# A decoder step on one core: ten of sixteen expert column blocks as a dense product, the sample's weighted rows spread over the picking, the last layer norm tile by tile

## The chip, the cores and the metric

The kernel runs on one core of one Trainium2 chip. The metric is the device time of one launch in microseconds, the median of several runs. The profile is one further execution, recorded by the hardware profiler; its span is the time from the first to the last instruction of the program.

The core has five engines with instruction streams of their own: TensorE (PE; its weight loads are listed apart as PEld), VectorE (DVE), ScalarE (ACT), GpSimd (POOL) and SyncE (SP). Each works through its stream in order and waits on semaphores for the others. SP's stream issues plain transfers; POOL's issues the gathers, in which a list of 128 row numbers picks 128 rows of a table.

## The reference

One layer of a decoder for a prompt of 256 tokens and a sample of 8 x 4 = 32 tokens: an input projection, an RWKV head group and a sparse-attention head group, an output projection with layer norm, and then the channel mixer, a product-key expert layer (PEER) with a second layer norm. The change lies in the last part:

```python
hv, hix = lax.top_k(s, P_TOPK)
cand = (hv[:, :, 0, :, None] + hv[:, :, 1, None, :]).reshape(n, P_HEADS, P_TOPK * P_TOPK)
cand_e = (hix[:, :, 0, :, None] * N_KEYS + hix[:, :, 1, None, :]).reshape(n, P_HEADS, P_TOPK * P_TOPK)
tv, tpos = lax.top_k(cand, P_TOPK)
expert = jnp.take_along_axis(cand_e, tpos, axis=-1)
gate = jax.nn.softmax(tv, axis=-1).astype(x.dtype)
...
h = jax.nn.gelu(jnp.einsum('cd,chkd->chk', xb, u_tab[eb]), approximate=False)
return jnp.einsum('chk,chkd->cd', gb * h, v_tab[eb])
```

Each token picks 8 heads x 16 = 128 of 16384 experts. For each it needs the dot product of its row (2048 columns) with the expert's row of `peer_u`, a GELU, a gate, and the sum of the experts' rows of `peer_v` with these weights. The result is added to the token and normed: `layer_norm(DEEPNORM_ALPHA * x + f, ln2_g, ln2_b)`.

## The kernel before

The first 1200 us or so compute everything up to the choice of the experts, and the sample's own dot products; the change leaves them as they are. Tile sizes are written into the code. A planner of the framework orders the instructions of each engine by a timeline of its own, with priorities in the order of the program; instructions passed to `pin` (`tc.keep_in_program_order`) keep their order among themselves, and `tc.issue_after(i)` lets an instruction be issued only after `i`. A pool's named tile with `bufs=n` has n buffers in turn: a new tile waits until the one n before has been read for the last time. Memory of a closed pool goes to later pools, and the first writer of a new tile waits for the last reader of what lay there.

Four stages follow for the prompt's 256 tokens.

**Dense** (`dense`, lines 1873 to 1888, called 128 times from line 1891). The 2048 columns of `peer_u` are split in 16 column blocks of 128. The last `NDB` = 9 are multiplied for all 16384 experts and all tokens on TensorE, in 128 blocks of 128 experts: `ph` (128 experts x 256 tokens) sums over the nine column blocks. Three of them (`NSP` to `NDB`) are plain f32 matmuls with `Xfd` (line 1879), which run in two passes, with two weight loads and two matmuls each. The other six (`SPLIT`, in two groups of three) are split into a high part `uh`, cast on ACT (line 1639), and a rest `ul`, made on DVE (line 1640), and take three matmuls each with the split tokens `XHd`, `XLd` (line 1886). ACT then copies `ph` into the table `AW` (line 1888). A block's weights `ur` come with one transfer of 576 KB.

The other seven column blocks (`UG` = 896 columns) are not multiplied densely: for each prompt tile `t` (128 tokens) and each of a token's 128 choices, `fetch` (line 1789) gathers the 128 chosen rows, cut to 896 columns, into one of the five `rows` buffers (`NRW`), and `dot` (line 1797) multiplies them with the tokens on DVE and sums (line 1803): 256 dot products. Two of them are done before the dense stage; in each block of it `n_` = 1 or 2 follow the block's last `ul`, `NDN` = 4 of 8 blocks having the second. `table` (line 1808) lays the finished sums and the experts' numbers down by token in `TB`.

**Picking** (from line 1993, 68 steps `s_`, all pinned but for the transfers and the last norm). A step takes four tokens. `pick` compares the experts' numbers with a row of counts (`oo`, DVE, line 1918) and transposes one half on TensorE (`pt`, line 1922; ACT copies it, line 1924); `picked` takes the dense sums with it from `AW` (`px`, line 1930); one step later `product_of` reduces them on DVE to the chosen experts' sums (four small passes, line 1941), every second step adds the gathered part (line 1944) and ACT takes the GELU (line 1945); then the gate (`gated`, DVE, line 1949), three steps later the scaling (`scaled`, ACT, line 1955), and four steps later `put`, which multiplies the weights out into a dense table of 256 tokens x 16384 experts (`pa`, line 1963) that ACT writes over `AW` (line 1964). The dot products left over from the dense stage are spread over the steps 0 to 27.

In the steps 28 to 59 `smp_fetch` gathers the sample's rows of `peer_v`, two halves of 4 KB a row, into two of the same five `rows` buffers, and two steps later (30 to 61) `smp_add` multiplies them with the sample's weights `ws` into `fs`: four matmuls of 32 output rows and 512 columns, in two passes (line 1982). 32 such products make the sample's sum. After the steps the sample's sum is added to its tokens and normed in `norm_quarters` (lines 2027, 2028 and 1444 to 1459: statistics on DVE, a small matmul `avg4`, an inverse root in some ten small DVE steps, one pass on ACT and two on DVE), and 16 small transfers on SP's queue store it.

**V** (lines 2063 to 2106). The weights in `AW` are multiplied with the first `FD` = 1408 columns of `peer_v`, in 128 row blocks `k`. Each is loaded by `rows_load` on SP's queue (three buffers: every third one in the pool `vr`, the others in `vp`, which lies where the dot products' and the picking's tiles lay), split on ACT and DVE into `vh` and `vl` (two buffers each), and multiplied for both prompt tiles `t` into six banks `acc` in 18 matmuls. The other 640 columns are gathered (`row_fetch`) and summed on DVE (`row_add`, line 2058). Row block 0 is loaded at step 50 of the picking, the blocks 1 and 2 after it.

**End** (lines 2109 to 2133). `last_sum` adds the banks and the gathered part to the tokens and takes statistics; then both tiles' mean and inverse root are made together (13 small steps), and for each of the eight pieces of 512 columns ACT scales and shifts, DVE multiplies with `ln2_g` and adds `ln2_b`, and SP stores.

## Time and profile before

| | |
|---|---|
| median of 3 runs | 2496.15 us (2490.72 to 2497.42) |
| the profiled execution | 2498.71 us |
| its span | 2496.9 us |
| PE busy | 2246.1 us (90%) |
| DVE busy | 1851.9 us (74%) |
| POOL busy | 1373.4 us (55%) |
| ACT busy | 927.4 us (37%) |
| moved by DMA | 684.23 MB, 274 GB/s |

Times in rows are counted from the start of the span. A row of the timeline gives start, duration, engine, line, operation and the tiles written and read; `x6` means six such instructions in a row, and the brackets at its end give the idle time of the engine ahead of it and what ended it. Rows of the stretches give the busy time of each engine in a stretch, with the number of instructions in brackets, the TensorE clock granted (1.00 is full speed), the busy share of the DMA engines and what they moved. Matmuls overlap in their pipeline, so a busy TensorE need not be one at its peak: how far their starts lie apart tells more. A group's row gives line, engine, operation, tiles, shapes and number, then busy time and the mean in ns of one, then the idle time before it.

### The profile page before, as it was taken

The numbers are of one execution on the slowest core, as the hardware profiler recorded it, in microseconds if no ns is written. First come the engines' busy times: TensorE is split into PE (matmuls) and PEld (weight loads), VectorE is DVE, ScalarE is ACT, GpSimd is POOL, SyncE is SP. The second block draws the span as 40 slices with busy tenths as digits, with TensorE's granted clock in tenths as the row PEclk, the third lists the DMA queues.
The fourth block names the chain that finished last, engine by engine and source line by source line (L and its number), as shares of the span: only waits on it lengthen the run. The fifth ranks groups of instructions, "written<-read, shape, count | busy, mean of one in ns | idle before, by whom it ended". The sixth has DMA issues, their size and how long they took to land.

```text
span 2496.9 us, 44823 instructions
## 1 busy us (share of the span) xinstructions
PE 2246.1 (90%) x16396; PEld 1888.6 (76%) x16396; DVE 1851.9 (74%) x4241; ACT 927.4 (37%) x1848; POOL 1373.4 (55%) x1422
## 2 busy tenths in 40 slices
PE   7979999988889997789699999996699799999996
PEld 7967898875545665678598889986676688888785
DVE  5789756554563446889977776779976799988888
ACT  4433222213441333220233343434566444443433
POOL 5677423242444005478655555556656488876662
PEclk9999999998896896899899999997899899999998
DMA  7777975457668884797499999996678599999995
GB/s 219 234 235 232 272 220 172 122 178 223 214 206 269 283 299 148 282 325 241 144 385 372 370 361 357 353 336 221 216 249 294 221 369 356 362 365 361 350 358 186
DMA packets 327613, 684.23 MB, mean 274 GB/s; under 512 B 82270, under 2 KB 200992, under 8 KB 326464
## 3 DMA queue, kind: packets, MB, share of 16 engines
q1 hardware_dynamic: 246176, 342.58, 41.4%
q0 software_dynamic: 81216, 338.78, 38.4%
q8 instruction: 129, 2.11, 0.3%
q14 instruction: 92, 0.75, 0.1%
HBM read 665.69 MB, written 23.88 MB: 276 GB/s over the span
## 4 chain that ended last, share of the span: by engine, by line
PE 60%; DVE 17%; DMA 8%; issue 7%; ACT 4%; POOL 3%; SPq 1%; DVEq 0%; POOLq 0%; ACTq 0%
PE pb L2085 17%; PE ph L1886 10%; PE pj L426 8%; PE ph L1879 3%; PE pa L1668 3%; PE p L1083 2%; DVE rows L1803 2%; DMA co<-in_cache_cmp_kv,gidx 2%; DVE sr L1559 2%; PE pa L1963 2%; DVE ul L1640 2%; PE ss L1500 1%; PE px L1930 1%; PE fs L1982 1%; DVE oo L1918 1%
## 5 line engine op out<-in xcount | busy, mean ns | idle before, releaser
L457 POOL DMA_INDIRECT rows<-in_peer_u_g,gi x256 | 332.3, 1298 | 239.5 <-DVE rows L1803 195.2
L457 POOL DMA_INDIRECT rq<-in_peer_v_g,gi x256 | 378.6, 1479 | 141.8 <-DVE fP L2058 80.2
L1803 DVE SCALAR_TENSOR_TENSOR rows<-rows,x1a 128x896 f32<-128x896 f32 x256 | 272.0, 1092 | 2.9 <-DMA rows<-in_peer_u_g,gi 2.7
L1886 PE MATMUL ph<-XHd,ul 128*128 128x256 f32 x768 | 225.3, 294 | 27.6 <-DVE ul L1640 22.7
L426 PE MATMUL pj<-XH,wl 128*128 128x288 f32 (+1 forms) x752 | 230.1, 306 | 15.2 <-DVE wl L421 9.1
L426 PE MATMUL pj<-XH,wh 128*128 128x288 f32 (+1 forms) x752 | 228.2, 304 | 13.6 <-DVE ss L756 6.9
L1886 PE MATMUL ph<-XHd,uh 128*128 128x256 f32 x768 | 236.7, 308 | 0.0
L2058 DVE SCALAR_TENSOR_TENSOR fP<-rq,ge,fP 128x640 f32<-128x640 f32 x254 | 223.8, 881 | 5.9 <-DMA rq<-in_peer_v_g,gi 3.4
L426 PE MATMUL pj<-XL,wh 128*128 128x288 f32 (+1 forms) x752 | 224.5, 299 | 0.0
L1640 DVE TENSOR_TENSOR ul<-ur,uh 128x384 fp32r<-128x384 f32 x256 | 131.8, 553 | 120.1 <-ACT uh L1639 93.3
L1886 PE MATMUL ph<-XLd,uh 128*128 128x256 f32 x768 | 217.4, 283 | 0.0
L2085 PE MATMUL pb<-vl,ah 128*128 128x512 f32 (+1 forms) x768 | 207.8, 378 | 1.4 <-issue 0.5
L2085 PE MATMUL pb<-vh,ah 128*128 128x512 f32 (+1 forms) x768 | 188.0, 380 | 20.9 <-ACT vh L2077 20.9
L2085 PE MATMUL pb<-vh,al 128*128 128x512 f32 (+1 forms) x768 | 205.7, 376 | 0.0
L419 ACT CAST wh<-wraw 128x512 fp32r<-128x512 f32 (+1 forms) x188 | 114.7, 617 | 223.7 <-PE pj L426 169.0
L1879 PE MATMUL ph<-Xfd,ur 128*128 128x256 f32 x768 | 187.6, 380 | 1.1 <-DMA ur<-in_peer_u_t 1.1
L1886 PEld LDWEIGHTS ph<-XHd,ul 128*128 128x128 f32 x768 | 147.0, 192 | 42.1 <-DVE ul L1640 41.8
L2085 PEld LDWEIGHTS pb<-vh,ah 128*128 128x128 f32 x768 | 145.5, 196 | 43.8 <-ACT vh L2077 24.5
L480 DVE SCALAR_TENSOR_TENSOR CA<-co,wbc,CA 128x256 f32<-128x256 f32 x248 | 133.9, 577 | 45.5 <-DMA co<-in_cache_cmp_kv,gidx 45.2
L2085 PEld LDWEIGHTS pb<-vl,ah 128*128 128x128 f32 x768 | 145.2, 195 | 24.5 <-DVE vl L2078 4.5
L426 PEld LDWEIGHTS pj<-XH,wl 128*128 128x128 f32 (+1 forms) x752 | 142.6, 190 | 26.6 <-DVE wl L421 12.7
L1888 ACT COPY AW<-ph 128x256 f32<-128x256 f32 x128 | 77.8, 608 | 228.1 <-PE ph L1886 198.7
(854 smaller groups left out, 5472.6 us busy)
## 6 DMA issues: line engine op xcount, KB each, us to landing
ur<-in_peer_u_t SPq DMA_DIRECT2D x128, 576.0 KB
wraw<-in_w_in SPq DMA_DIRECT2D x152, 256.0 KB
cw<-in_w_out SPq DMA_DIRECT2D x32, 512.0 KB
wraw<-in_w_out SPq DMA_DIRECT2D x32, 512.0 KB
wraw<-in_peer_wq SPq DMA_DIRECT2D x32, 512.0 KB
cw<-in_peer_wq SPq DMA_DIRECT2D x32, 512.0 KB
wraw<-in_w_in SPq DMA_DIRECT2D x64, 128.0 KB
co<-in_state_win_kv SPq DMA_DIRECT2D x16, 512.0 KB
```

The source lines that it names most:

```text
L419: sc.copy(wh[:, :, :n], w[:, :, :n])
L426: last[2] = pe.matmul(pb[:n, :nt], wi[:, k, :n], xi[(o + k) // 8][:, (o + k) % 8, :nt], start=(o + k == 0 and wi is wh and xi is xh), stop ...
L457: gp.indirect_dma_start(out=dst, out_offset=None, in_=rows_, in_offset=bass.IndirectOffsetOnAxis(ap=ix, axis=0))
L480: ve.scalar_tensor_tensor(d_, x_, w_, d_, op0=OP.mult, op1=OP.add)
L1640: return ve.tensor_tensor(xl, pb, xh.bitcast(F32), OP.subtract)
L1668: pe.matmul(acc[t], xi[:, e, P * t:P * t + P], wi[:, e, :], start=(k == e == n_ == 0), stop=(k == 6 and e == 1 and n_ == 2))
L1803: i_ = ve.scalar_tensor_tensor(r_, r_, 1.0, X1a[t], op0=OP.mult, op1=OP.mult, accum_out=h_)
L1879: pe.matmul(ph[:, :NPR], w[:, e, :], Xfd[:, e - NSP, :], start=(e == NSP), stop=False)
L1886: mm = pe.matmul(ph[:, :NPR], wi[:, e - e0, :], xi[:, e, :], start=False, stop=(e == NSP - 1 and wi is wl))
L1888: return lo_, mm, sc.copy(AW[:, i1 // 64, :, i1 % 64], ph[:, :NPR])
L2058: ve.scalar_tensor_tensor(fP[t], r_, w_, fP[t], op0=OP.mult, op1=OP.add)
L2085: pe.matmul(acc[3 * t + q][:, :n_], wi[:, P * t:P * t + P], xi[:, 512 * q:512 * q + n_], start=(k == 0 and wi is ah and xi is vh), stop=(k ...
```

## The change

Five edits, all in the expert layer:

- `NDB` is 10: ten column blocks are multiplied densely, four of them plain, and the gathered rows are `UG` = 768 columns. A block's transfer is 640 KB.
- `NDN` is 6: six of eight blocks of the dense stage have a second dot product. Of the tile `uh` there are two buffers instead of three.
- In the picking's steps 0 to 27 the rows of a dot product are fetched at most two ahead (`ahead=2`), not five. The sample's 32 products stand at the steps 5, 6, 8, 10, 12, 13 and so on to 59, four in seven steps, and their fetches two steps ahead of each. The loads for the sample's norm move from step 46 to 44.
- The sample's sum, norm and stores stand in the program behind step 61 instead of after the picking.
- In V the last two row blocks are multiplied together, first both for tile 0 and then both for tile 1. The last norm makes mean and inverse root for each tile on its own, and each piece takes two operations on DVE, (x - mean) x g and that x the inverse root + b, and none on ACT.

```diff
-NDN = 4
+NDN = 6
...
-NDB = 9
+NDB = 10
...
-            wh, wl = (dp([P, e1 - e0, P], nm, F32R, bufs=3) for nm in ("uh", "ul"))
+            wh, wl = (dp([P, e1 - e0, P], nm, F32R, bufs=n_) for nm, n_ in (("uh", 2), ("ul", 3)))
...
+    turns = {5 + j * 7 // 4: j for j in range(32)}
...
-            dot(-(-left * (s_ + 1) // 28) + 2 * P - left - got[1], keep=True)
-        elif s_ < 60:
-            smp_fetch(s_ - 28)
-        if 30 <= s_ < 62:
-            smp_add(s_ - 30)
-        if s_ == 46:
+            dot(-(-left * (s_ + 1) // 28) + 2 * P - left - got[1], keep=True, ahead=2)
+        if s_ + 2 in turns:
+            smp_fetch(turns[s_ + 2])
+        if s_ in turns:
+            smp_add(turns[s_])
+        if s_ == 44:
...
+        if s_ == 61:
+            ve.scalar_tensor_tensor(x_, x_, ALPHA, fs, op0=OP.mult, op1=OP.add)
+            norm_quarters(x4p, x_, gs_, bs_, "pb")
+            for q in range(4):
+                for i in range(4):
+                    sy.dma_start(outs[1][:, i, 512 * q:512 * q + 512], x_[32 * q + 8 * i:32 * q + 8 * i + 8, :])
...
-    ve.scalar_tensor_tensor(x_, x_, ALPHA, fs, op0=OP.mult, op1=OP.add)
-    norm_quarters(x4p, x_, gs_, bs_, "pb")
-    for q in range(4):
-        for i in range(4):
-            sy.dma_start(outs[1][:, i, 512 * q:512 * q + 512], x_[32 * q + 8 * i:32 * q + 8 * i + 8, :])
...
+        parts[k] = (ah, al, vh, vl)
         for t in range(2):
-            for wi, xi in ((ah, vh), (ah, vl), (al, vh)):
...
+            for k_ in (k,) if k < P - 2 else (k - 1, k) if k == P - 1 else ():
+                ah, al, vh, vl = parts[k_]
+                for wi, xi in ((ah, vh), (ah, vl), (al, vh)):
...
     for t in range(2):
         for q in range(3):
             last_sum(t, q)
+        v_, r_ = v2[:, t:t + 1], rr2[:, t:t + 1]
         ve.bn_aggr(out=mv2[:, t, :], in_=sf[:, t].rearrange("p a b -> p (a b)"))
-    m_, v2 = mv2[:, :, 0], vp([P, 2], "v2")
-    ve.tensor_scalar(v2, mv2[:, :, 1], 1e-5, None, op0=OP.add)
-    rsqrt(vp, rr2, v2, "ln2")
-    ve.scalar_tensor_tensor(v2, m_, -1.0, rr2, op0=OP.mult, op1=OP.mult)
-    for t in range(2):
-        for q in range(4):
-            c_ = slice(512 * q, 512 * q + 512)
-            x_ = xo[t][:, c_]
-            sc.activation(x_, x_, AF.Identity, bias=v2[:, t:t + 1], scale=rr2[:, t:t + 1])
-            ve.tensor_tensor(x_, x_, g2_[:, c_], OP.mult)
-            ve.tensor_tensor(x_, x_, b2_[:, c_], OP.add)
+        ve.tensor_scalar(v_, mv2[:, t, 1:2], 1e-5, None, op0=OP.add)
+        m_ = mv2[:, t, 0:1]
+        ve.tensor_scalar(m_, m_, -1.0, None, op0=OP.mult)
+        xs_ = [(xo[t][:, 512 * q:512 * q + 512], slice(512 * q, 512 * q + 512)) for q in range(4)]
+        rsqrt(vp, r_, v_, f"ln2{t}")
+        for x_, c_ in xs_:
+            ve.scalar_tensor_tensor(x_, x_, m_, g2_[:, c_], op0=OP.add, op1=OP.mult)
+            ve.scalar_tensor_tensor(x_, x_, r_, b2_[:, c_], op0=OP.mult, op1=OP.add)
             sy.dma_start(outs[0][0, t * P:(t + 1) * P, c_], x_)
```

More of the change, by code (lines that the diff above doesn't have):

```diff
@@ L2060, in row_add @@
             ve.tensor_scalar(fP[t], r_, w_, None, op0=OP.mult)
-    acc = [bank() for _ in range(6)]
+    acc, parts = [bank() for _ in range(6)], {}
     done = 0
@@ L2080, in hybrid_decode_step @@
             ld_ = rows_load(k + 3)
+        parts[k] = (ah, al, vh, vl)
         for t in range(2):
-            for wi, xi in ((ah, vh), (ah, vl), (al, vh)):
-                for q in range(3):
-                    n_ = min(512, FD - 512 * q)
-                    pe.matmul(acc[3 * t + q][:, :n_], wi[:, P * t:P * t + P], xi[:, 512 * q:512 * q + n_],
-                              start=(k == 0 and wi is ah and xi is vh), stop=(k == P - 1 and wi is al))
+            for k_ in (k,) if k < P - 2 else (k - 1, k) if k == P - 1 else ():
+                ah, al, vh, vl = parts[k_]
+                for wi, xi in ((ah, vh), (ah, vl), (al, vh)):
+                    for q in range(3):
+                        n_ = min(512, FD - 512 * q)
+                        pe.matmul(acc[3 * t + q][:, :n_], wi[:, P * t:P * t + P], xi[:, 512 * q:512 * q + n_],
+                                  start=(k_ == 0 and wi is ah and xi is vh), stop=(k_ == P - 1 and wi is al))
         while done < min(len(queue), len(queue) * (k + 1) // (P - 2)):
@@ L2117, in hybrid_decode_step @@
     last_sum(1, 3)
+    v2 = vp([P, 2], "v2")
     for t in range(2):
```

## The prediction

> **What bounds the kernel now.** I read the stretches first (columns: stretch and length; busy time and instructions of PE, PEld, DVE, ACT, POOL; granted TensorE clock; DMA share; GB/s), because the change touches three stages with different limits.
>
> ```profile
> 1250.00:1675.00 425.00, 420.15 (x2807) 383.92 (x2806) 304.24 (x607) 165.55 (x350) 238.62 (x185) 1.00 0.98 365
> 1682.00:1815.00 133.00, 89.92 (x532) 82.82 (x531) 127.91 (x396) 60.87 (x164) 81.40 (x63) 0.78 0.70 219
> 1820.00:1940.00 120.00, 119.00 (x938) 85.29 (x938) 83.00 (x339) 81.34 (x223) 67.83 (x59) 1.00 0.78 266
> ```
>
> The dense stage (first row) is TensorE's: 2807 matmuls, 24 an expert block (three plain columns in two passes each, 18 of the split kind), are 117 blocks in 425 us, 3.63 us a block. The first 28 steps of the picking (second row) are VectorE's, busy 127.9 of 133 us, and TensorE runs there at a clock of 0.78. The other steps (third row) are TensorE's again, 119 of 120 us at full clock, with VectorE at 83. So a column moved to TensorE is paid in the first row, the dot products it shortens are earned in the second, and the sample's products, which fill the third, can be moved into the second.
>
> **The dense stage.** The timeline, PEld, ACT and DVE rows around two blocks:
>
> ```profile
> 1472.13 1.18 PEld L1879 LDWEIGHTS ph<-Xfd,ur 128*128 128x128 f32 x6
> ...
> 1473.66 0.19 PEld L1886 LDWEIGHTS ph<-XHd,ul 128*128 128x128 f32 x1
> ...
> 1475.57 1.18 PEld L1879 LDWEIGHTS ph<-Xfd,ur 128*128 128x128 f32 x6
> ...
> 1475.89 0.59 ACT L1888 COPY AW<-ph 128x256 f32<-128x256 f32 x1 [2.83 <-PE ph L1886]
> 1476.28 0.93 ACT L1639 CAST uh<-ur 128x384 fp32r<-128x384 f32 x2
> 1476.84 1.03 DVE L1640 TENSOR_TENSOR ul<-ur,uh 128x384 fp32r<-128x384 f32 x2 [2.07 <-ACT uh L1639]
> ...
> 1477.45 0.19 PEld L1886 LDWEIGHTS ph<-XHd,ul 128*128 128x128 f32 x1 [0.27 <-DVE ul L1640]
> ...
> 1479.36 1.17 PEld L1879 LDWEIGHTS ph<-Xfd,ur 128*128 128x128 f32 x6
> ```
>
> One block takes 3.44 us (1472.13 to 1475.57), the next 3.79. In the short one the first `ul` product comes 1.53 us after the block's start, in the long one 1.88: ACT evacuates the block before, only then casts `uh`, DVE then makes `ul`, and TensorE, through with its three plain columns, waits. Six weight loads in 1.18 us make a plain column 0.39. The fourth one therefore costs 0.39 us of work, but it stands ahead of the wait: TensorE reaches the first `ul` at 1.53 + 0.39 = 1.92, when `ul` is there (1.88). Every block then takes 3.44 + 0.39 = 3.83, against 3.63 on average: +0.20 x 128 = **+26 us**. Bounds: not below this (no block takes less than the short one and the fourth column's work), and 0.39 x 128 = +50 if each wait stays as long as it is. The cover is thin, 0.04 us. I take +26.
>
> `uh` with two buffers instead of three: the cast of a block's second half now waits until the second half of the block before has been multiplied, some 0.1 us before that block ends. Behind it on ACT stands at most the evacuation, and `ul` of the second half is wanted nine products of 0.12 us after the 1.92: over 2 us of room, so nothing. DVE: two `ul` (1.03) and 1.75 dot products instead of 1.5, each shorter: under 2.8 of 3.83 us. DMA: a block's load grows from 590 to 655 KB, the rows from 1.5 x 459 to 1.75 x 393 KB: 1343 KB in 3.83 us is 351 GB/s, against 365 in the row. Nothing. Of the 256 dot products two are done before this stage and 1.5 x 128 in it, so 62 are left for the picking; with 1.75 x 128 it is 30.
>
> **The first 28 steps of the picking.** VectorE's timeline, whose second row shows where one step begins and the last where the next does; below them step 28's pick, and the page's groups of two row sizes:
>
> ```profile
> 1682.25 1.22 DVE L1918 TENSOR_TENSOR oo<-CT,TB 128x1024 f32<-128x1024 f32 x1
> ...
> 1701.26 1.22 DVE L1918 TENSOR_TENSOR oo<-CT,TB 128x1024 f32<-128x1024 f32 x1
> ...
> 1703.81 1.08 DVE L1803 SCALAR_TENSOR_TENSOR rows<-rows,x1a 128x896 f32<-128x896 f32 x1
> ...
> 1704.82 1.09 DVE L1803 SCALAR_TENSOR_TENSOR rows<-rows,x1a 128x896 f32<-128x896 f32 x1
> ...
> 1706.84 1.22 DVE L1918 TENSOR_TENSOR oo<-CT,TB 128x1024 f32<-128x1024 f32 x1
> ```
> ```profile
> 1815.62 1.22 DVE L1918 TENSOR_TENSOR oo<-CT,TB 128x1024 f32<-128x1024 f32 x1
> ```
> ```profile
> L1803 DVE SCALAR_TENSOR_TENSOR rows<-rows,x1a 128x896 f32<-128x896 f32 x256 | 272.0, 1092 | 2.9 <-DMA rows<-in_peer_u_g,gi 2.7
> L2058 DVE SCALAR_TENSOR_TENSOR fP<-rq,ge,fP 128x640 f32<-128x640 f32 x254 | 223.8, 881 | 5.9 <-DMA rq<-in_peer_v_g,gi 3.4
> ```
>
> A step without dots is 2.55 us (1701.26 to 1703.81), a dot 1.01 start to start. 28 x 2.55 + 62 x 1.01 = 134.0 against 133.4 measured (1682.25 to 1815.62): the account closes. A dot of 768 elements lies midway between 896 and 640, 0.105 us less: 0.91. After: 28 x 2.55 + 30 x 0.91 = 98.7.
>
> Fourteen of the 32 sample products now fall into these steps. TensorE, in a steady step of today's second part:
>
> ```profile
> 1874.15 0.66 PE L1922 MATMUL pt<-CT,oo 128*128 128x128 f32 x4
> 1874.64 1.06 PE L1963 MATMUL pa<-oo 128*128 128x128 f32 x8
> 1875.54 1.16 PE L1930 MATMUL px<-AW,oT 128*128 128x128 f32 x8
> 1876.63 1.06 PE L1982 MATMUL fs<-rows,ws 128*32 128x512 f32 x8
> 1877.62 0.66 PE L1922 MATMUL pt<-CT,oo 128*128 128x128 f32 x4
> ```
>
> 3.47 us with a sample product, 0.99 of it that product, 2.48 without. The 28 steps ask 28 x 2.48 + 14 x 0.99 = 83.3 us of TensorE, under VectorE's 98.7. As the limits are now close I add what today's second part loses against its sum: 33 steps from 1819.82 to the last pick (1940.33, below) are 3.65 each, not 3.47, 5%: 103.6, **-30 us**. Bounds: -35 without that loss, and the rivals.
>
> **The other steps.**
>
> ```profile
> 1819.82 1.22 DVE L1918 TENSOR_TENSOR oo<-CT,TB 128x1024 f32<-128x1024 f32 x1 [0.43 <-PE pa L1963]
> ```
> ```profile
> 1940.33 1.22 DVE L1918 TENSOR_TENSOR oo<-CT,TB 128x1024 f32<-128x1024 f32 x1
> ```
>
> From step 28 to the last pick 124.7 us pass. After, 18 of these 35 steps hold a sample product (3.47) and 17 fall to VectorE's 2.55 (ACT's 81.3 us over the 33 steps are 2.46 each, just below): 105.8, with 5% 111: **-14**, bounds -19 and 0, the last if the four engines, all near 2.5 in a short step, keep each other waiting.
>
> **The start of the last stage.**
>
> ```profile
> 1952.42 0.81 ACT L1457 ACTIVATE x1a<-x1a,smv,srr 128x512 f32<-128x512 f32 x1 [0.94 <-DVE smv L1442]
> ...
> 1954.71 6.01 SPq L2031 DMA_DIRECT2D out<-x1a  x16
> ...
> 1961.09 0.37 SPq L1990 DMA_DIRECT2D v__20899<-in_peer_v  x1
> ...
> 1962.79 0.96 POOL L457 DMA_INDIRECT rq<-in_peer_v_g,gi  x1 [30.07 <-DMA out<-x1a]
> ...
> 1967.30 2.10 PEld L2085 LDWEIGHTS pb<-vh,ah 128*128 128x128 f32 x6 [5.94 <-ACT vh L2077]
> ```
>
> Sixteen stores of the sample's result stand on SP's queue ahead of the second row block's load, which leaves at 1961.09; TensorE waits 5.9 us for it. The sample's sum and norm now follow step 61, two steps after the last sample product (step 59), so the stores should be issued while the picking ends, and the load be back in time. What is late next is the cast of the first block, which today stands on ACT behind the sample's scaling at 1952.42: some 2 us earlier. Against this, the norm's VectorE work (four passes of 512, some twenty small steps, near 6 us, part of which runs among the picks already) and its one small product on TensorE, which waits for VectorE with the next transposes and puts behind it, now stand among steps 61 to 65: +2. Net **-6**, bounds 0 (the scheduler leaves the norm late) and -10.
>
> **The end.**
>
> ```profile
> 2479.78 0.38 DVE L2121 BATCH_NORM_AGGREGATE mv<-sf 128x2 f32<-128x24 f32 x2
> ...
> 2483.61 1.40 DVE L2131 TENSOR_TENSOR AW<-AW 128x512 f32<-128x512 f32 x2 [0.88 <-ACT AW L2130]
> ...
> 2490.94 2.49 DVE L2132 TENSOR_TENSOR AW<-AW 128x512 f32<-128x512 f32 x4
> ```
> ```profile
> 1967.00:2474.00 507.00, 494.12 (x2285) 430.31 (x2286) 456.89 (x455) 212.65 (x189) 375.35 (x253) 1.00 0.95 352
> ```
>
> VectorE closes this: 16 passes from 2483.61 to 2493.43, before them 2.95 us of small steps and 0.88 of waiting for ACT. In the last stage a matmul takes 494.12 / 2285 = 0.216 us, a tile's nine 1.9. Multiplied tile by tile, tile 0 is whole up to one such turn earlier (if the last block's casts, now wanted a turn earlier, come in time); the wait for ACT goes (-0.9); but the small steps, now for each tile, are done twice (+2.8) and the 16 passes stay 16. -1.9 - 0.9 + 2.8 = **0**, bounds -3 and +3.
>
> **Sum.** 26 - 30 - 14 - 6 + 0 = -24. The profiled execution took 2498.7 us (span 2496.9), 2.6 over the median; against the median, 2496.15 - 24 = **2472 us**. With the better bounds it is 26 - 35 - 19 - 10 - 3 = -41, 2455.
>
> **Rivals.** *The column is paid in full.* If a dot stands before `ul` on VectorE, the wait in front of `ul` moves along with the column: +50 in place of +26, 2496. For it: the 0.04 us of cover. Against it: in the row at 1476.84 VectorE had been idle for 2.07 us. 0.12.
>
> *The shared row buffers.* Dots and sample rows now take turns in five buffers, and a row's gather waits in POOL's one queue for the buffer five back, at times for a sample product at the end of the very step before its use; behind it wait all later gathers. The latency of one gather:
>
> ```profile
> 1691.22 1.09 DVE L1803 SCALAR_TENSOR_TENSOR rows<-rows,x1a 128x896 f32<-128x896 f32 x1 [1.08 <-DMA rows<-in_peer_u_g,gi]
> ```
>
> Here VectorE stood 1.08 us for a row. At one such place per sample product, 15 x 1.1 = +16 less what the 5% hold already: about 2485. Counting through the buffers I find it at one place in seven steps, so 0.17.
>
> *The clock.* Now the slower side: with its filling thinned out in the second part, and gaps left in the first, TensorE could get there the clock that it gets now in the first, 0.78. The work, 83.3 + 104.6 us at full clock, would take 241 in place of 258: -17, so 26 - 17 - 6 = +3, 2499; at 0.70 it is 268, +30, 2526. It decides below 0.79. Against it: a TensorE that slows becomes the bound, is busy without gaps, and the third row of the first fence shows such a stretch at 1.00. 0.11. [...]
>
> *The change doesn't do what it says*: the norm isn't run among the picks, or the steps keep their order of waits; -6 and some of -14 are missing, 2485. 0.05.
>
> **How the numbers follow.** Forecast 0.55 (2455 to 2482), buffers 0.17, full column 0.12, clock 0.11, misplaced norm 0.05. About 0.3%, 7.5 us, is what a measurement of this kernel can tell from no change, so faster means below 2488.6: forecast, buffers and misplaced norm, 0.77. Within 0.3%: 0.09 of the full column and 0.04 of the clock, 0.13. Slower: 0.03 of the full column, with a worse term beside it, and 0.07 of the clock, 0.10. The range goes from 2455, the better bounds, to 2494; outside stay the clock, half of the full column and 0.03 below.
>
> **What would show it.** Dense: plain weight loads in eights, 3.83 us apart, and no PEld wait for `ul`; 4.1 would be the first rival. Picking: first 28 steps near 104 us with VectorE still busiest, TensorE's clock over 0.9; waits of dots for their gathers would be the second rival. The rest near 111 us in two kinds of steps. The second row block's load leaving before the first is multiplied. Wrong altogether if the two gains of the picking don't come to over 26 us together.

## The result and the profile after

The changed kernel takes 2508.4 us (median of 12 runs, 2498.9 to 2517.4) against 2492.8 of the kernel before (12 runs, 2474.2 to 2498.0): a ratio of 1.0077, interval 1.0058 to 1.0095. It is slower by 0.8%; the forecast was 1% faster. The profiled execution took 2508.9 us, with a span of 2507.1.

The two profiles, cut at the same marks (first plain weight load of the dense stage, last block's, picks 0, 28 and 63, last multiplication of V):

| stretch | before, us | after, us | forecast | measured |
|---|---|---|---|---|
| up to the dense stage | 1189.9 | 1178.9 | | (-11.0) |
| its first 17 blocks | 87.6 | 101.1 | +26 in all | +13.5 |
| its other 110 blocks | 401.2 | 427.6 | | +26.4 |
| last block to pick 0 | 3.5 | 5.3 | | +1.7 |
| first 28 steps | 133.4 | 134.7 | -30 | +1.3 |
| other steps | 124.7 | 113.6 | -14 | -11.1 |
| last pick to V's last multiplication | 534.2 | 523.8 | -6 | -10.4 |
| end | 22.4 | 22.1 | 0 | -0.3 |
| sum without the first row | 1307.0 | 1328.1 | -24 | +21.1 |

The first row is no effect of the change: over the profiles of this study it lies between 1170.4 and 1200.2 us, at nine columns 1184.0 to 1198.4 and at ten 1170.4 to 1200.2. So stretches are compared here, and sums without it; the 21.1 is 0.8% of the whole, as the ratio says.

The stretches of the changed kernel (columns as in the prediction's first fence): dense stage, step 0, steps 1 to 27, the others, V.

```profile
1275.00:1700.00 425.00, 425.00 (x2851) 401.70 (x2850) 281.46 (x598) 168.09 (x329) 192.87 (x188) 1.00 0.95 344
1713.00:1728.00 15.00, 3.88 (x14) 2.79 (x14) 10.84 (x24) 0.59 (x1) 12.12 (x10) 0.53 0.86 280
1728.00:1847.00 119.00, 83.62 (x628) 65.62 (x628) 89.33 (x324) 60.53 (x164) 71.99 (x56) 0.94 0.69 217
1850.00:1960.00 110.00, 102.13 (x820) 81.02 (x819) 86.77 (x357) 80.97 (x223) 41.44 (x33) 1.00 0.54 167
1976.00:2484.00 508.00, 496.25 (x2299) 432.56 (x2299) 458.19 (x458) 212.96 (x189) 376.31 (x254) 1.00 0.95 351
```

The third row is the surprise: in 119 us VectorE is busy for 89 and TensorE for 84. Before, VectorE filled this stage (127.9 of 133). The dots did get fewer and shorter, but no engine bounds the stage any more: something is waited for. The page's group of the dots says what:

```profile
L1803 DVE SCALAR_TENSOR_TENSOR rows<-rows,x1a 128x768 f32<-128x768 f32 x256 | 244.8, 962 | 31.0 <-DMA rows<-in_peer_u_g,gi 27.1
```

Before, 2.9 us of idle time stood in front of the dots in the whole kernel; now it is 31.0, and 27.1 of it ended with the gather of a row. The view of waits in steps 1 to 27 (total us, times, longest) shows who waits for whom:

```profile
POOL rows L457 <- DVE rows L1803: 31.3, 17, 2.6
...
DVE rows L1803 <- DMA rows<-in_peer_u_g,gi: 19.2, 12, 3.6
```

A circle: POOL waits for dots to free row buffers, dots wait for POOL's gathers. One turn of it, on POOL (`in_peer_u_g` is a dot's row, `in_peer_v` a half of a sample row), then on VectorE and on TensorE:

```profile
1779.10 0.95 POOL L457 DMA_INDIRECT rows<-in_peer_v,gi  x1 [0.30 <-issue]
1781.59 1.69 POOL L457 DMA_INDIRECT rows<-in_peer_v,ig  x1 [1.53 <-DVE rows L1803]
1783.59 0.95 POOL L457 DMA_INDIRECT rows<-in_peer_u_g,gi  x1 [0.30 <-PE pa L1963]
...
1789.66 1.69 POOL L457 DMA_INDIRECT rows<-in_peer_v,gi  x1 [2.60 <-DVE rows L1803]
...
1796.73 1.69 POOL L457 DMA_INDIRECT rows<-in_peer_u_g,gi  x1 [2.07 <-PE fs L1982]
```
```profile
1783.78 0.95 DVE L1803 SCALAR_TENSOR_TENSOR rows<-rows,x1a 128x768 f32<-128x768 f32 x1
...
1788.43 0.96 DVE L1803 SCALAR_TENSOR_TENSOR rows<-rows,x1a 128x768 f32<-128x768 f32 x1 [3.68 <-issue]
```
```profile
1795.11 1.34 PE L1982 MATMUL fs<-rows,ws 128*32 128x512 f32 x8
```

The sample's gather at 1781.59, the second half of the row begun at 1779.10, waited 1.53 us for a dot. Behind it in POOL's queue stood the gather of the next dot, which left at 1783.59; the dot ran at 1788.43, 4.84 us later, after 3.68 us in which VectorE did nothing (the view calls the wait "issue", but the buffer it reads is the one gathered at 1783.59). At 1796.73 it is a dot's gather that waits, 2.07 us, for a sample product (the one at 1795.11) to free its buffer. Thirteen dots of steps 1 to 27 wait like this, 22.9 us together: the 19.2 above and this 3.68.

Step 0 is the second surprise, 15.0 us in place of 4.3:

```profile
1712.82 1.22 DVE L1918 TENSOR_TENSOR oo<-CT,TB 128x1024 f32<-128x1024 f32 x1
...
1717.45 0.96 DVE L1803 SCALAR_TENSOR_TENSOR rows<-rows,x1a 128x768 f32<-128x768 f32 x1 [1.52 <-DMA rows<-in_peer_u_g,gi]
...
1721.74 0.96 DVE L1803 SCALAR_TENSOR_TENSOR rows<-rows,x1a 128x768 f32<-128x768 f32 x1 [1.30 <-DMA rows<-in_peer_u_g,gi]
...
1727.85 1.22 DVE L1918 TENSOR_TENSOR oo<-CT,TB 128x1024 f32<-128x1024 f32 x1
```

Ten dots stand between the first two picks, two of the picking's thirty and eight of the dense stage's, and TensorE has little to do (3.9 of 15 us in the second row above).

The dense stage in the changed kernel (PEld), and the start of V (SP's queue, then PEld):

```profile
1501.14 1.61 PEld L1879 LDWEIGHTS ph<-Xfd,ur 128*128 128x128 f32 x8
...
1505.02 1.61 PEld L1879 LDWEIGHTS ph<-Xfd,ur 128*128 128x128 f32 x8
```
```profile
1958.74 5.82 SPq L2028 DMA_DIRECT2D out<-x1a  x16
1964.92 0.37 SPq L1990 DMA_DIRECT2D v__21027<-in_peer_v  x1
```
```profile
1975.46 1.17 PEld L2090 LDWEIGHTS pb<-vh,ah 128*128 128x128 f32 x6 [2.67 <-ACT ah L2076]
```

Behind the first 17 blocks nearly every block takes 3.88 us, and none waits for `ul`. The second row block's load leaves at 1964.92, 10.5 us ahead of the first multiplication; before, it left 6.0 us behind it.

### The profile page after: what moved, and what is told of

It reads as the page before. It is cut to its first block, busy times and chain, and to the rows that moved or that the text cites. A ratio compares the mean times of both kernels' runs of the same rounds, so it can differ in the third digit from the quotient of the medians.

```text
span 2507.1 us, 45293 instructions
## 1 busy us (share of the span) xinstructions
PE 2257.3 (90%) x16652; PEld 1919.0 (77%) x16652; DVE 1828.2 (73%) x4254; ACT 933.7 (37%) x1840; POOL 1328.2 (53%) x1422
## 4 chain that ended last, share of the span: by engine, by line
PE 63%; DVE 13%; DMA 10%; issue 5%; POOL 5%; ACT 2%; SPq 1%; DVEq 0%; POOLq 0%; ACTq 0%
PE pb L2090 19%; PE ph L1886 10%; PE ph L1879 8%; PE pj L426 7%; DMA rows<-in_peer_u_g,gi 3%; PE pa L1668 2%; DVE sr L1559 2%; PE p L1083 2%; DMA co<-in_cache_cmp_kv,gidx 2%; DMA big<-in_state_rwkv 2%; PE pa L1963 1%; PE px L1930 1%; PE ss L1500 1%; PE pt L1922 1%; DVE CA L480 1%
## 5 line engine op out<-in xcount | busy, mean ns | idle before, releaser
L457 POOL DMA_INDIRECT rows<-in_peer_u_g,gi x256 | 272.3, 1064 | 283.8 <-DVE rows L1803 257.1
L1803 DVE SCALAR_TENSOR_TENSOR rows<-rows,x1a 128x768 f32<-128x768 f32 x256 | 244.8, 962 | 31.0 <-DMA rows<-in_peer_u_g,gi 27.1
L1640 DVE TENSOR_TENSOR ul<-ur,uh 128x384 fp32r<-128x384 f32 x256 | 142.1, 557 | 157.6 <-ACT uh L1639 157.6
L1879 PE MATMUL ph<-Xfd,ur 128*128 128x256 f32 x1024 | 245.0, 382 | 4.0 <-DMA ur<-in_peer_u_t 4.0
L1639 ACT CAST uh<-ur 128x384 fp32r<-128x384 f32 x256 | 130.9, 513 | 309.1 <-PE ph L1886 288.3
L426 PE MATMUL pj<-XH,wl 128*128 128x288 f32 (+1 forms) x752 | 231.5, 308 | 13.5 <-DVE wl L421 7.8
L1886 PE MATMUL ph<-XHd,ul 128*128 128x256 f32 x768 | 218.5, 285 | 23.9 <-DVE ul L1640 23.9
L1879 PEld LDWEIGHTS ph<-Xfd,ur 128*128 128x128 f32 x1024 | 187.1, 192 | 25.8 <-DMA ur<-in_peer_u_t 4.7
L426 PEld LDWEIGHTS pj<-XH,wl 128*128 128x128 f32 (+1 forms) x752 | 144.4, 192 | 24.1 <-DVE wl L421 11.1
```

Source lines behind the costliest of these rows:

```text
L426: last[2] = pe.matmul(pb[:n, :nt], wi[:, k, :n], xi[(o + k) // 8][:, (o + k) % 8, :nt], start=(o + k == 0 and wi is wh and xi is xh), stop ...
L457: gp.indirect_dma_start(out=dst, out_offset=None, in_=rows_, in_offset=bass.IndirectOffsetOnAxis(ap=ix, axis=0))
L1639: sc.copy(xh, pb)
L1640: return ve.tensor_tensor(xl, pb, xh.bitcast(F32), OP.subtract)
L1803: i_ = ve.scalar_tensor_tensor(r_, r_, 1.0, X1a[t], op0=OP.mult, op1=OP.mult, accum_out=h_)
L1879: pe.matmul(ph[:, :NPR], w[:, e, :], Xfd[:, e - NSP, :], start=(e == NSP), stop=False)
```

## The experiments

"A" is the theory that dots and sample rows take each other's row buffers, "B" that the eight left-over dots hold up step 0, "C" that clock or contention does it, "D" that the two `uh` buffers slow the first blocks of the dense stage. All runs, with the sum of their profile behind the first row of the table above (before: 1307.0):

| run | ratio to before, interval | first 28 steps, us | sum, us |
|---|---|---|---|
| changed kernel | 1.0077, 1.0058 to 1.0095 | 134.7 | 1328.1 |
| e1_dense_only | 1.0077, 1.0045 to 1.0110 | 110.7 | 1319.4 |
| e2_spread_only | 1.0237, 1.0202 to 1.0272 | 204.4 | 1355.9 |
| e3_after_ahead5 | 1.0149, 1.0105 to 1.0192 | 141.4 | 1337.6 |
| e4_after_late | 1.0058, 1.0034 to 1.0082 | 112.0 | 1318.2 |
| e5_after_one | 1.0034, 1.0011 to 1.0056 | 118.7 | 1313.6 |
| e6_spread_one | 1.0087, 1.0060 to 1.0113 | 172.5 | 1325.7 |
| e7_uh2_only | 1.0036, 1.0011 to 1.0062 | 132.6 | 1310.8 |
| e8_norm_early | 0.9975, 0.9953 to 0.9996 | 132.5 | 1300.1 |
| e9_best9 | 0.9995, 0.9972 to 1.0018 | 133.6 | 1299.7 |
| e10_best8 | 0.9974, 0.9948 to 1.0000 | 140.2 | 1298.7 |
| e11_after_one5 | 1.0251, 1.0213 to 1.0289 | 137.1 | 1361.8 |
| e12_norm_end | 0.9982, 0.9957 to 1.0007 | 132.6 | 1299.7 |

### Ten columns alone

Against the kernel before:

```diff
-NDN = 4
+NDN = 6
-NDB = 9
+NDB = 10
-            wh, wl = (dp([P, e1 - e0, P], nm, F32R, bufs=3) for nm in ("uh", "ul"))
+            wh, wl = (dp([P, e1 - e0, P], nm, F32R, bufs=n_) for nm, n_ in (("uh", 2), ("ul", 3)))
```

> Only the tenth column goes to TensorE (with the two uh buffers it needs); the sample's sums, the norm and the end stay as before, so the ring of five row buffers serves dots alone in the first 28 steps and dots are fetched five ahead. Theory A (in the changed kernel the sample's rows in the dots' ring make the dots wait): without them the first 28 steps fall to what VectorE's sum says, 28 x 2.55 + 38 dots x 0.91 = 106, plus the 5 us of gaps that before had: 106 to 111 us, and the kernel is 28.9 + 1.7 (dense stage, first pick) - 25 = +5 us, ratio 1.000 to 1.005. Theory B (the eight dots left over from the dense stage choke step 0 by themselves): step 0 stays at 15 us with its waits, first 28 steps 110 to 115. Theory C (a slower granted TensorE clock or contention of the gathers, not the ring): the first 28 steps stay near 134 us and the kernel is 30 us slower, ratio 1.012.

The stretches step 0 and steps 1 to 27:

```profile
1731.00:1746.00 15.00, 3.67 (x14) 2.58 (x14) 10.45 (x22) 0.59 (x1) 12.25 (x10) 0.55 0.81 268
1746.00:1841.00 95.00, 66.50 (x510) 60.76 (x511) 89.20 (x326) 58.94 (x160) 47.24 (x30) 0.96 0.43 130
```

VectorE does the same work as in the changed kernel, 89.2 us, but in 95 us instead of 119, and no dot of steps 1 to 27 waits for its gather. These steps take 95.2 us; VectorE's account of the prediction, 27 x 2.55 + 28 x 0.91, gives 94.3. So A holds for 24 us, and B holds too: step 0 takes 15.45 us with no sample row anywhere near. C is not quite settled by this run: the sample's gathers, and what they might do to the others, are gone from the stage along with the sharing, and dots are fetched five ahead instead of two. e3 and e5 below keep those gathers. The whole is slower than expected, since the dense stage costs +36.7 (first 17 blocks 97.9, the others 427.6), not the +28.9 that I had read from two times on the clock, with the first row of the table in them.

### The spread sums alone

Against the changed kernel; `uh` has three buffers and the end is as before, too:

```diff
-NDN = 6
+NDN = 4
-NDB = 10
+NDB = 9
...
```

> The sample's sums are spread over the picking, dots are fetched two ahead and the norm follows step 61, as in the changed kernel; nine columns on TensorE and the end stay as before. Theory A (shared ring): 62 dots of 1.01 keep VectorE at 134 us in the first 28 steps, and the waits of dots for gathers that stand behind a sample row's add 15 to 30 us: 150 to 165. The other steps take 114 as in the changed kernel (-11), the last stage -10: together between -5 and +10 us, ratio 0.998 to 1.004. Theory C (no harm by the ring; the waits of the changed kernel come from its dense stage's left-over dots): first 28 steps 134 to 138, and the kernel is 17 to 21 us faster, ratio 0.992 to 0.993.

Waits of the first 28 steps:

```profile
POOL rows L457 <- DVE rows L1803: 67.8, 37, 3.9
DVE rows L1803 <- DMA rows<-in_peer_u_g,gi: 58.4, 20, 5.4
```

With 62 dots in the ring instead of 38 the same edit costs 71 us (204.4 against 133.4) where 15 to 30 were expected: a miss in size, in A's direction. The other steps (113.7) and V (510.8) are as in the changed kernel.

### The lead of the dots

Against the changed kernel:

```diff
-            dot(-(-left * (s_ + 1) // 28) + 2 * P - left - got[1], keep=True, ahead=2)
+            dot(-(-left * (s_ + 1) // 28) + 2 * P - left - got[1], keep=True)
```

> The changed kernel, with dots fetched five ahead as before instead of two. If the short lead of two dots is what makes them wait (theory A1), the first 28 steps fall from 134.7 towards 106 to 115 us and the kernel is 20 to 28 us faster than the changed one, ratio to the kernel before 0.997 to 1.000. If five buffers are too few for dots and sample rows together whatever the lead (theory A2), a row's gather still waits for the use of the buffer five back: first 28 steps 125 to 145 us, ratio 1.004 to 1.012. If the left-over dots at step 0 are the matter (theory B), step 0 keeps its 15 us and the rest of the steps stay as they are.

A2 by these steps (141.4 us, inside its 125 to 145), though the ratio, 1.0149, is above its 1.012. Waits of steps 1 to 27:

```profile
DVE xj L1941 <- PE px L1930: 22.6, 7, 6.7
...
PE fs L1982 <- DMA rows<-in_peer_v,gi: 14.1, 9, 2.4
...
PE fs L1982 <- DMA rows<-in_peer_v,ig: 8.6, 11, 1.4
```

No dot waits for its gather any more. Instead the sample rows come late: TensorE waits 22.7 us for them (14.1 + 8.6), in its fixed order the picks stand behind that, and VectorE waits 22.6 us for TensorE. Fetching the one kind of row earlier only moved the wait to the other here.

### The sums put back

Against the changed kernel:

```diff
-            dot(-(-left * (s_ + 1) // 28) + 2 * P - left - got[1], keep=True, ahead=2)
-        if s_ + 2 in turns:
-            smp_fetch(turns[s_ + 2])
-        if s_ in turns:
-            smp_add(turns[s_])
+            dot(-(-left * (s_ + 1) // 28) + 2 * P - left - got[1], keep=True)
+        if 28 <= s_ < 60:
+            smp_fetch(s_ - 28)
+        if 30 <= s_ < 62:
+            smp_add(s_ - 30)
...
-        if s_ == 61:
+        if s_ == 63:
```

> The changed kernel, with the sample's sums put back to steps 30 to 61, where no dot shares the ring, and the norm after step 63. Theory A (shared ring): first 28 steps 106 to 111 us, other steps back at 125, last stage still 8 to 10 shorter than before since the norm's stores leave early: 28.9 + 1.7 - 25 + 0 - 9 = -3 us against the kernel before, ratio 0.997 to 1.001. Theory C (clock or contention): first 28 steps stay at 134, ratio 1.008 to 1.012. Theory B (left-over dots): step 0 alone still 12 to 15 us, first 28 steps 110 to 115.

First 28 steps 112.0, step 0 alone 15.1, other steps 122.8, V 511.5 with 18.7 us before it: A and B once more. The total missed (+11 in the sum, not -3): the dense stage costs 8 us more than the 28.9, as in the first run, and the early norm brings 4 us, not 9, between the last pick and the end of V.

### A shorter hold

Against the changed kernel:

```diff
-        if s_ + 2 in turns:
-            smp_fetch(turns[s_ + 2])
         if s_ in turns:
             smp_add(turns[s_])
+        lead = 1 if s_ < 27 else 2
+        for n_ in (1, 2):
+            if s_ + n_ in turns and n_ <= lead and (turns[s_ + n_], 0) not in sr:
+                smp_fetch(turns[s_ + n_])
```

> The changed kernel, but in the first 27 steps a sample row is fetched one step ahead instead of two, and only after the sample product of its step is issued, so that it holds its two ring buffers for one step less. Theory A (a dot's gather waits for the buffer of a sample row that is still waiting for its product): most of the 24 us by which the first 28 steps exceed those of the run without sharing (134.7 against 110.7) go, first 28 steps 112 to 122 us, the kernel 13 to 22 us faster than the changed one, ratio to the kernel before 0.998 to 1.003. Rival (a row's latency is what counts, whoever holds the buffer): TensorE now waits for the sample row that has only one step, and the first 28 steps stay at 130 to 140, ratio 1.006 to 1.010.

118.7 us, as A said: 16 of the 24 us are won back when sample rows hold their buffers for one step less. The edit also puts a sample row's gather behind the product of its step, so hold and order aren't told apart. Waits and stretch, 1742 to 1845:

```profile
DVE rows L1803 <- DMA rows<-in_peer_u_g,gi: 5.7, 5, 1.3
```
```profile
1742.00:1845.00 103.00, 89.37 (x606) 66.78 (x607) 89.68 (x326) 58.16 (x158) 72.48 (x55) 0.92 0.74 240
```

This settles C. POOL issues as many gathers here (55, busy 72.5 us) as in steps 1 to 27 of the changed kernel (56, 72.0 us), the DMA engines are busier (0.74 against 0.69) and the clock is no higher (0.92 against 0.94), yet the steps take 16 us less. Neither traffic nor clock made the waits.

The same edit in the version with the spread sums alone, with nine columns:

```diff
-        if s_ + 2 in turns:
-            smp_fetch(turns[s_ + 2])
...
+        lead = 1 if s_ < 27 else 2
...
```

> Nine columns as before, the sample's sums spread over the picking with rows fetched one step ahead as in the run before this one, the norm after step 61. Theory A: the first 28 steps fall from the 204 us of the version with two steps' lead to VectorE's 134 plus a few waits, 136 to 150; other steps 114 and last stage 510 as there, so 2 to 15 us less than the kernel before at 136 to 145, ratio 0.993 to 1.002. Rival (five buffers are too few for 62 dots and 28 sample rows whatever the order): 170 to 205 us, ratio 1.010 to 1.024.

172.5 us, between the version with two steps' lead (204.4) and VectorE's 134: here the rival has it by the steps (170 to 205), while the ratio, 1.0087, lies between the two forecasts. With 59 dots and 28 sample rows in 27 steps, five buffers are too few in this order too; a single lead does not decide it. Separate buffers for the sample rows would be the clean test; it wasn't tried.

### Two buffers for uh

Against the kernel before:

```diff
-            wh, wl = (dp([P, e1 - e0, P], nm, F32R, bufs=3) for nm in ("uh", "ul"))
+            wh, wl = (dp([P, e1 - e0, P], nm, F32R, bufs=n_) for nm, n_ in (("uh", 2), ("ul", 3)))
```

> The kernel before with two uh buffers in place of three, nothing else. The first 17 blocks of the dense stage took 84 to 88 us with nine columns and three buffers, and 98 to 101 us in all four kernels with ten columns and two; 4 of these 13 us are the fourth column's own. Theory D (with two uh buffers fewer casts stand ready when VectorE comes back from its selection work): the first 17 blocks take 93 to 97 us here, the 110 blocks behind them stay at 401, ratio 1.003 to 1.004. Rival (the longer loads of ten columns and TensorE's work make it): 84 to 88 us, ratio 0.999 to 1.001.

The first plain weight loads of block 1 and of block 18, in the kernel before and in this one:

```profile
1189.90 1.17 PEld L1879 LDWEIGHTS ph<-Xfd,ur 128*128 128x128 f32 x6
...
1277.47 1.18 PEld L1879 LDWEIGHTS ph<-Xfd,ur 128*128 128x128 f32 x6
```
```profile
1192.09 1.17 PEld L1879 LDWEIGHTS ph<-Xfd,ur 128*128 128x128 f32 x6
...
1287.06 1.18 PEld L1879 LDWEIGHTS ph<-Xfd,ur 128*128 128x128 f32 x6
```

95.0 us against 87.6, inside D's range, and the 110 blocks behind them stay at 399.9. The edit that I had put at nothing costs 7 us at the start of the stage, and the ratio of 1.0036 agrees. VectorE is away there at the selection, and TensorE waits 22.1 us for one `ul` before and 21.4 in this version. The loss lies in the 13 blocks behind that wait: 51.0 us before, 59.2 here. Which wait in them makes it was not followed.

### The norm among the picks

Against the kernel before, sum, norm and stores moved:

```diff
         if s_ == 50:
             rows_load(0)
+        if s_ == 63:
+            ve.scalar_tensor_tensor(x_, x_, ALPHA, fs, op0=OP.mult, op1=OP.add)
+            norm_quarters(x4p, x_, gs_, bs_, "pb")
...
```

> The kernel before with the sample's sum, norm and sixteen stores moved into the picking, behind step 63, nothing else. If the changed kernel's 10 us in the last stage come from the second row block's load that no longer waits behind the stores, the last stage (first to last multiplication) takes 510 to 512 us in place of 519.5, and the time between the last pick and it grows by 0 to 4 as in the run with late sums: -5 to -9 us, ratio 0.996 to 0.998. If they come from elsewhere: no change, ratio 0.999 to 1.001.

V takes 510.3 us instead of 519.5, and 18.5 instead of 14.75 lie before it. SP's queue and PEld:

```profile
1951.35 5.95 SPq L2027 DMA_DIRECT2D out<-x1a  x16
1957.66 0.37 SPq L1990 DMA_DIRECT2D v__20899<-in_peer_v  x1
```
```profile
1961.30 2.10 PEld L2086 LDWEIGHTS pb<-vh,ah 128*128 128x128 f32 x6 [2.89 <-ACT vh L2078]
```

The load is issued 3.6 us ahead of the first multiplication, and the 5.94 us that TensorE waited for the second row block are gone. The other 3 of V's 9 us are not traced to one wait. This version is faster than before, by 0.04 to 0.5%, and faster than the changed kernel.

Against the kernel before, with the sums two steps earlier and the norm behind step 61:

```diff
-        elif s_ < 60:
-            smp_fetch(s_ - 28)
-        if 30 <= s_ < 62:
-            smp_add(s_ - 30)
+        if 26 <= s_ < 58:
+            smp_fetch(s_ - 26)
+        if 28 <= s_ < 60:
+            smp_add(s_ - 28)
...
+        if s_ == 61:
```

> Nine columns and three uh buffers as before, the sample's sums at steps 28 to 59 (two earlier than before, so behind the last dot but for the first four rows' gathers), norm and stores behind step 61 instead of step 63; no tile-by-tile end. The run with the norm behind step 63 alone kept the last stage at 510 us but paid 3.7 us between the last pick and that stage (18.5 against 14.75). Theory: two steps earlier the norm's waits lie inside the picking as in the changed kernel (14.3), so dense stage and first 28 steps as before, other steps 124 to 127, 14 to 15, last stage 509 to 511: 7 to 11 us less than before, ratio 0.9955 to 0.9975. Rival: the norm's 4 us only move into the other steps (128 to 130): ratio 0.997 to 0.999.

The rival: 14.3 us before V and V at 509.5, but the other steps at 128.3. In both places the norm takes some 4 us; the profile's sum is the same as that of the run before (1299.7 and 1300.1), and the ratio can't be told from 1.

### Eight columns

Against the version before this one:

```diff
-NDB = 9
+NDB = 8
```

> The kernel of the run before this one with eight columns on TensorE instead of nine: the change's first edit in the other direction. Theory E (a block's length is TensorE's own work): 0.39 us less a block, 110 blocks 401 - 43 = 358 us; the first 28 steps, whose 62 dots get 1024 elements wide, 133 + 62 x 0.13 = 141: 35 to 40 us faster than the run before it. Rival (the chain of the evacuation, the cast to uh and the subtraction to ul sets the block once the plain columns in front of it are fewer): blocks of 3.6 to 3.8, 110 blocks 396 to 417, first 28 steps 141: 5 us faster to 25 us slower than the run before it.

Blocks of this version (PEld):

```profile
1451.22 0.74 PEld L1879 LDWEIGHTS ph<-Xfd,ur 128*128 128x128 f32 x4
1454.24 0.74 PEld L1879 LDWEIGHTS ph<-Xfd,ur 128*128 128x128 f32 x4
1455.54 0.19 PEld L1886 LDWEIGHTS ph<-XHd,uh 128*128 128x128 f32 x1 [0.55 <-ACT uh L1639]
1456.13 0.19 PEld L1886 LDWEIGHTS ph<-XHd,ul 128*128 128x128 f32 x1 [0.30 <-DVE ul L1640]
1458.04 0.74 PEld L1879 LDWEIGHTS ph<-Xfd,ur 128*128 128x128 f32 x4
```

A block without a wait takes 3.02 us, one with waits for `uh` and `ul` 3.80, as long as with nine columns (3.79). 110 blocks take 392.6 us, 9 less than with nine columns instead of 43: the rival. With the dots 1024 wide (140.2) it comes out level, 1298.7 against 1299.7.

### Fewer dots in the dense stage

Against the version with the shorter hold:

```diff
-NDN = 6
+NDN = 5
```

> The changed kernel with the one-step lead, and with 13 dots in eight blocks of the dense stage instead of 14, so 46 dots are meant for the picking instead of 30. With 14, eight of the dense stage's dots were run behind the first pick, and step 0 took 15 us in every kernel with ten columns. Theory B (the dots that the dense stage can't take up are queued together there): step 0 falls to 4 to 6 us, 8 dots more are spread over the steps: first 28 steps 118.7 - 10 + 8 x 0.95 = 116, and up to 8 more for waits in the fuller ring; ratio to the kernel before 1.001 to 1.006. Rival (step 0 is held up by the start of the picking with ten columns, not by these dots): step 0 stays at 13 to 15 and the first 28 steps grow to 126.

Step 0 falls to 2.9 us, with two dots in it: the eight queued dots were what made it long. But the first 28 steps take 137.1 us instead of the expected 116, 18 more than with `NDN` = 6. 47 dots stand in them instead of 38, and in the steps 1 to 27 twelve dots now wait 19.9 us in all (the row below and 6.5 us for TensorE), where four waited 4.7 us in the version before (the fifth in its row belongs to step 0):

```profile
DVE rows L1803 <- DMA rows<-in_peer_u_g,gi: 13.4, 10, 3.2
```

And the dense stage grows by 28 us (110 blocks 455.7 instead of 427.6; the last 34 of them take 4.8 us each). VectorE late in it:

```profile
1692.86 0.56 DVE L1640 TENSOR_TENSOR ul<-ur,uh 128x384 fp32r<-128x384 f32 x1 [2.61 <-ACT uh L1639]
1693.34 0.95 DVE L1803 SCALAR_TENSOR_TENSOR rows<-rows,x1a 128x768 f32<-128x768 f32 x1
...
1694.22 0.95 DVE L1803 SCALAR_TENSOR_TENSOR rows<-rows,x1a 128x768 f32<-128x768 f32 x1
...
1695.10 0.55 DVE L1640 TENSOR_TENSOR ul<-ur,uh 128x384 fp32r<-128x384 f32 x1
```

Two dots now stand between the `ul` of a block's two halves, 2.24 us apart, and VectorE waits for the next cast. Some of TensorE's waits there are for the block's own load `ur`, too (20.0 us from 1600 to 1722). Why the order came out so, and what it would cost with three `uh` buffers, is open.

### The two harmless parts together

Against the kernel before with the norm behind step 63, the last two row blocks tile by tile and the last norm in two operations:

```diff
+            for k_ in (k,) if k < P - 2 else (k - 1, k) if k == P - 1 else ():
+                ah, al, vh, vl = parts[k_]
...
+            ve.scalar_tensor_tensor(x_, x_, m_, g2_[:, c_], op0=OP.add, op1=OP.mult)
+            ve.scalar_tensor_tensor(x_, x_, r_, b2_[:, c_], op0=OP.mult, op1=OP.add)
...
```

> The kernel before with the two parts of the change that take nothing from the rows' ring and leave the nine columns: norm and stores behind step 63, and the last two row blocks multiplied tile by tile with the last norm in two operations. From the end I expect what the changed kernel showed, 22.0 to 22.1 us behind the last multiplication in place of 22.4; from the norm the 5 to 6 us that it gave alone: ratio 0.996 to 0.999. If the tile-by-tile end works against the early load in the last stage (a rival that nothing so far speaks for): last stage back above 515, ratio 1.000.

End 21.8 us instead of 22.4, V 511.6: as expected. The sum is 0.4 us below that of the norm alone, and the interval reaches to 1.0007: the end's 0.6 can't be told from nothing.

## Why the forecast was wrong

**The failed step: the first 28 steps, -30 forecast, +1.3 measured.** The sum of VectorE's work was right for the steps 1 to 27: e1 shows it to 1 us without the 5% that I had added for near limits. What failed is that the sum put the waits for row buffers at nothing beyond these 5%. I left them to a rival, "the shared row buffers", which I priced at "one place in seven steps" and +16 less the 5%, and gave 0.17. They came at 13 places of 1.8 us, since I counted buffers in the program's order and missed the circle: a sample row holds two of five buffers until its product, later gathers queue behind the one that waits, and each dot so delayed (4.84 us from gather to use in the turn above) delays the release that the next gather waits for. Taking sharing away gives 24.0 us back (134.7 to 110.7), fetching the sample rows later (e5) 16. Nor do the buffers go strictly in turn there, as the text on the kernel has it: the sample's gather at 1789.66 started behind a dot's release, while the row gathered five places ahead of it, at 1779.10, was not used before 1795.11. How the buffers were handed out stays open.

**Left-over dots.** "With 1.75 x 128 it is 30" counted the program, not the order on VectorE: eight more were run behind the first pick and step 0 took 15.0 us. Without sharing the first 28 steps stand 7.1 us above the forecast's 103.6: step 0 is 12 longer than a step of that sum, less the unneeded 5%. Together 24.0 + 7.1 = 31.1, the whole miss of this term. Of the 12, some 7 are the eight dots' own work (8 x 0.91) and most of the rest waits for their gathers (4.0 us, four waits). Spread over the steps of the shared ring they cost more, not less (e11: 137.1 us for the first 28 steps against 118.7).

**The dense stage, +26 forecast, about +41.6 measured.** The mechanism was right: behind the first blocks no wait for `ul` is left and nearly all blocks are alike, at 3.88 us instead of 3.83. The column costs 0.43 (blocks without a wait take 3.02, 3.45 and 3.88 us with eight, nine and ten columns), not 0.39: I divided 1.18 us by three, where the difference of two rows, 1.61 - 1.18, is the price. A block grows by 0.24 on average (427.6 / 110 - 401.2 / 110) instead of 0.20, over 128 blocks by 31. "So nothing" for the two `uh` buffers was wrong by 7: I looked at the steady stage, not at its start. 1.7 went into the first pick. These add to 39.7; some 2 us of the first blocks are not accounted for; the wait for the selection in them, the longest for `ul`, differs by as much between profiles (22.1 us before, 21.4 in e7, 20.3 after, 19.6 in e4, 19.4 in e1).

**The rest held.** Other steps -11.1 (forecast -14, between its bounds). V and its start -10.4 at the bound of -10: the load does leave early, and e8 shows that this alone brings 9 us in V, while some 4 us of norm go into the picking or behind it, at either place that was tried (e8, e9). The end gave 0.3 (forecast 0).

**The other rivals.** The full column (+50) would show as waits for `ul` in every block; behind the first blocks there are none. The clock is not it: 0.94 in steps 1 to 27 after, against 0.78 in the first 28 steps before, and 1.00 in the other steps. "The change doesn't do what it says" is out, the norm runs among the picks.

So the gain was there and was given back twice: 24 us to the ring and 12 to step 0; and its price was 15 higher than forecast. Even e5, with most of the ring's loss mended, is slower than before; of the parts run alone only the early norm (e8) pays.

## What to carry to other kernels

Before two kinds of data share a ring of buffers, follow the ring as a circle: for each gather, which use frees its buffer (in the trace, not only by counting back), what stands behind it in the issuing queue, and how long after that its own user runs; a wait that appears "sometimes" can feed itself (13 dots waited 22.9 us here), and a longer lead only handed it to the other kind (in e3 TensorE waited 22.7 us for sample rows). When work is moved off an engine, look at the stage's start as well as at its steady state, and count the order on the engine rather than in the program. Take the price of one more item from the difference between two rows of the trace, not from a row divided by its count.

## What was not expected of the hardware

The TensorE clock granted in the first 28 steps is 0.78 before, with TensorE busy for 68% of the time (89.92 of 133), and 0.96 in steps 1 to 27 of e1, with 70% (66.50 of 95). The busy share misleads here, since slow instructions count longer (four transposes took 1.09 us in one step and 0.63 in another, below): e1 ran 510 matmuls in 95 us, the kernel before 532 in 133. More shows in the stretch before when it is taken in slices of 3.41 us, at whose borders the granted clock changes there. Four slices in a row:

```profile
1735.41:1738.82 3.41, 2.83 (x25) 2.64 (x25) 3.01 (x11) 2.55 (x9) 1.75 (x2) 1.00 0.77 219
1738.82:1742.24 3.42, 1.10 (x11) 0.94 (x10) 3.35 (x11) 1.19 (x6) 2.45 (x2) 1.00 0.60 203
1742.24:1745.65 3.41, 3.11 (x16) 2.82 (x14) 3.34 (x8) 2.43 (x7) 1.64 (x2) 0.50 0.68 238
1745.65:1749.06 3.41, 2.52 (x20) 2.33 (x20) 3.31 (x13) 2.01 (x6) 1.51 (x2) 1.00 0.73 210
```

In the second slice TensorE is busy for only 1.10 us, and the third has half the clock (0.50); TensorE is busy for 3.11 us of that one, and the fourth has the full clock again. From 1704.69 to 1813.92 there are twenty slices at full clock. After the ten in which TensorE was busy for 1.48 us or less the next slice had 0.50, after the ten with 1.84 us or more it had 1.00. So the pause just ahead of an instruction did not tell its pace here (PE):

```profile
1721.69 1.09 PE L1922 MATMUL pt<-CT,oo 128*128 128x128 f32 x4 [0.96 <-DVE oo L1918]
1732.10 1.09 PE L1922 MATMUL pt<-CT,oo 128*128 128x128 f32 x4 [3.32 <-DVE oo L1918]
1741.51 0.63 PE L1922 MATMUL pt<-CT,oo 128*128 128x128 f32 x4 [2.32 <-DVE oo L1918]
```

Four transposes behind 0.96 us took 1.09 us, and four behind 2.32 us took 0.63: they still ran in the second slice, ahead of the change at 1742.24. The slices are those of one stretch of one profile.
